# A decoder layer on one core: x given transposed too, weights laid out by chunks, plain x loaded later

## Chip, cores and metric

The kernel runs on one core of one Trainium2 chip. The metric is the device time of one execution in microseconds (us); several runs are made and their median is compared.

## What is computed

One layer with 256 positions and 1024 channels, all float32 at the interface. A pre-norm scales x by norm_in_g and by one over its root mean square; one wide projection w_in makes the inputs of two branches (block-sparse attention, which with 256 positions is plain causal attention of 8 heads, and gated linear attention, GLA), both are projected back, merged by sigmoid gates, projected by w_out, added to x and normed again.

```
h = rms_norm(x, norm_in_g)
(mq, mk, mv, mgate, gq, gk, gv, ggate, gfg, ga, gb) = split(h @ w_in)
oa = attention(rotary(mq), rotary(mk), mv) * silu(mgate);   ya = oa @ w_proj_a
ob = rms_norm(gla(gq/8, gk, gv, log_sigmoid(gfg @ w_fg2 + b_fg)/16)) * silu(ggate);   yb = ob @ w_proj_b
merged = sigmoid(ga + b_merge[0]) * ya + sigmoid(gb + b_merge[1]) * yb
out = rms_norm(x + merged @ w_out, norm_f_g)
```

## The kernel before

The 128 partitions hold channels (or positions), and every product keeps float32 precision by splitting both factors into a rounded part and a remainder (hi and lo for weights, xh and xl for x) and summing three matmuls: hi with xh, hi with xl, lo with xh. ScalarE makes each rounded part (a cast, line 179 for weights, line 256 for x), VectorE each remainder (line 180, line 257). The row's scale, one over the root mean square, is not applied to x but to the products' results.

Weights come in chunks in a fixed order (`load_to`, line 153; `split_to`, line 169). I call them by their product: **w0 to w7** are the eight chunks of the first product (the group "mg", kind K, 128 channels by 512 columns, 262 kB each, tile `first`), **g0 to g3** the four of the second ("gg", kind G, 541 kB each, tile `raw`), **q0 to q3** the four of the third ("gqk", 524 kB each), and so on. Raw chunks from g0 on have five buffers, hi and lo five each. x has eight pieces of 128 channels by 256 positions, **x0 to x7**.

All transfers of that stage are issued by SyncE's queue (SP), in program order. The framework gives the transfers eight counters in turn, so that a transfer is issued only once the one eight places before it has landed. x is loaded plain (positions on the partitions, tile `xt`), in rows of 512 bytes for x0 and x1 and of 1024 bytes later, ahead of the weight chunks that belong to them (lines 196 to 198). TensorE turns each piece by two transposes (`x_part`, line 252, tile `xp` in PSUM), and the casts read PSUM. norm_in_g arrives as rows and is turned by a transpose as well (tile `vp`, line 276), b_merge likewise in the middle of the second product (line 345).

The order of the instructions is written out by hand: the main loop over the groups (line 724) issues the products, and side generators such as `gates_mg` (line 338) are advanced at each `tick` when a clock that adds up matmul time says so. `squares` (line 266) sums the squares of x on ScalarE, `rms` (line 271) makes the row's scale `rs` on VectorE and GpSimd, `gates_mg` then makes two diagonal matrices of it (`diag`, line 343), broadcasts it over the partitions by matmuls with ones (line 349), copies the result to `rB` (line 351) and scales the first product by it (`mgz`, line 354). PSUM has four banks under the tag "small"; the third product's first bank, gqk, is the one that the first product's part mg0 leaves, so gqk's first matmul waits for the first `mgz` instruction, before and after the change.

Of the kernel before, what the change touches and what calls it, by code (L numbers as in the profile page):

```python
# [10 lines left out]
F32 = mybir.dt.float32  # L11
# [8 lines left out]
P = 128  # L20
# [55 lines left out]


@with_exitstack
def layer(ctx, tc, x, norm_in_g, w_in, b_merge, w_fg2, b_fg, gla_g, w_pa, w_pb, w_out, norm_f_g,
          rope, causal, sums, masks, out):  # L80
    nc = tc.nc
# [17 lines left out]
    def f32(ap):  # L99
        return ap.bitcast(F32)  # L100
# [9 lines left out]


    chunks = []
    groups = []

    def group(kind, name, src, c0, n, nk, step=2):
        ids = []
        if kind == "F":
            parts = [(c0 + p, 256, k0, 4) for p in range(0, n, 256) for k0 in range(0, nk, 4)]
        else:
            parts = [(c0, n, k0, step) for k0 in range(0, nk, step)]  # L120
        for c, w, k0, k in parts:
            ids.append(len(chunks))
            chunks.append(dict(src=src, c0=c, n=w, k0=k0, nk=k))
        groups.append(dict(kind=kind, name=name, ids=ids, nk=nk))

    group("K", "mg", w_in, C_MG, 512, KD, 1)
    group("G", "gg", w_in, C_GG, 528, KD)
    group("F", "gqk", w_in, C_GQ, 512, KD)
    group("F", "mq", w_in, C_MQ, 512, KD)
    group("F", "mk", w_in, C_MK, 512, KD)  # L130
    group("T", "mv", w_in, C_MV, 512, KD)
    group("T", "gv", w_in, C_GV, 512, KD)
    group("F", "ga0", w_in, C_GA, 512, KD)
    group("F", "ga1", w_in, C_GA + 512, 512, KD)
    group("F", "gb0", w_in, C_GB, 512, KD)
    group("F", "gb1", w_in, C_GB + 512, 512, KD)
    for h in range(2):
        group("F", f"pa{h}", w_pa, h * 512, 512, 4)
        group("F", f"pb{h}", w_pb, h * 512, 512, 4)
    oids = {}  # L140
    for half in range(2):
        for n in range(2):
            for k in range(4 * half, 4 * half + 4, 2):
                oids[n, k // 2] = len(chunks)
                chunks.append(dict(src=w_out, c0=n * 512, n=512, k0=k, nk=2))

# [6 lines left out]
    def load_to(n):  # L153
        while loaded[0] < min(len(chunks), n):
            c = chunks[loaded[0]]
            size = c["nk"] * c["n"]
            if loaded[0] < KD:
                c["raw"] = first[:, loaded[0], :]
            else:
                raw = ring.tile([P, WMAX], F32, name="raw", bufs=RAW)  # L160
                c["raw"] = raw[:, :size]
            nc.sync.dma_start(
                c["raw"].rearrange("p (k n) -> p k n", n=c["n"]),
                c["src"][c["k0"] * P:(c["k0"] + c["nk"]) * P, c["c0"]:c["c0"] + c["n"]].rearrange(
                    "(k p) n -> p k n", p=P),
            )
            loaded[0] += 1
# [38 lines left out]
    small_loads = [  # L206
        (brow, b_merge.rearrange("n (k p) -> (n k) p", p=P)),
        (flat(ropet), rope),
# [6 lines left out]
    ]  # L215
    load_to(KD + 2)
    for dst, src in small_loads[:6]:
        nc.sync.dma_start(dst, src)
# [44 lines left out]
    rB2 = rB[:, None, :].to_broadcast([P, 2, S])  # L263
    junk = one.tile([P, D], F32, name="junk", tag="m0")

    def squares(half):
        cs = slice(half * 512, half * 512 + 512)
        for t in range(NT):
            nc.scalar.activation(junk[:, :512], xt[:, t, cs], AF.Square, accum_out=ss[:, t, half:half + 1])

# [453 lines left out]
    for g in groups:  # L724
        ids, name = g["ids"], g["name"]
        if g["kind"] == "K":
            ps = [small(f"{name}{f}") for f in range(3)] + [bank(f"{name}3", "side", 1)]
            for i in ids:
                c = chunks[i]
                k = c["k0"]  # L730
                if k == 5:
                    squares(0)
                if k == 6:
                    squares(1)
                for f in range(4):
# [36 lines left out]
        elif g["kind"] == "F":  # L772
            src = {"pa": (oah, oal), "pb": (obh, obl)}.get(name[:2], (xh, xl))
            if name == "mq":
                for dst, given in small_loads[6:]:
                    nc.sync.dma_start(dst, given)
# [77 lines left out]
    for t in range(NT):  # L854
# [15 lines left out]

_INS = ["x", "norm_in_g", "w_in", "b_merge", "w_gla_fg2", "b_gla_fg", "gla_norm_g", "w_proj_a", "w_proj_b",
        "w_out", "norm_f_g"]
_ROWS = ("b_gla_fg", "gla_norm_g", "norm_f_g")


# [25 lines left out]
```

## Time and profile before

| what | value |
|---|---|
| median of 3 runs | 209.54 us (209.42 to 210.56) |
| the profiled execution | 209.73 us, its span 208.0 us |
| TensorE busy in the span | 198.8 us (96%) |
| VectorE, ScalarE busy | 141.6 us (68%), 122.6 us (59%) |
| moved by transfers | 35.39 MB, 170 GB/s over the span |

The span is the profiled part of that execution; 1.73 us of its time lie around it. Times in the rows further down are counted from the span's start. A matmul's busy time is modelled and overlaps the next one's, so the pace of TensorE is read from the distance of starts.

### The profile page before, as it was taken

Reading aid. Unit: us, or ns where it says so; the run is one execution under the profiler, and the core shown is the slowest. Engines: PE = TensorE matmul, PEld = TensorE weight load, DVE = VectorE, ACT = ScalarE, POOL = GpSimd, SP = SyncE. Lnnn points to the kernel's source line nnn. Section 1 sums busy time; section 2 is a strip of 40 time slices with the busy share of each in tenths; the row PEclk is TensorE's granted clock in tenths of the full one; section 3 lists DMA queues with packets and bytes.
Section 4 is the critical chain, followed back from the end, with each engine's and each line's share of the span. In section 5 each row is a group of like instructions: output and inputs, shape, how many; then the busy total and the mean of one; then the engine's idle time right before and its main releaser. Section 6 shows DMA issues by size and latency. Waiting matters only on the chain.

```text
span 208.0 us, 4231 instructions
## 1 busy us (share of the span) xinstructions
PE 198.8 (96%) x1683; PEld 182.4 (88%) x1683; DVE 141.6 (68%) x261; ACT 122.6 (59%) x205; POOL 32.5 (16%) x31
## 2 busy tenths in 40 slices
PE   7999999999999999998999999999999999999970
PEld 2899999899999988775789999999999999989870
DVE  1566778969545899989765556945393959755371
ACT  4369927871999984156775629846455554552251
POOL 2000025800214540103000000200010060420011
PEclk9999999999999999999999999999999999999998
DMA  5999896594364456660343563966344584600022
GB/s 144 349 379 323 238 310 211 135 296 149 101 199 117 145 158 191 193 218 14 107 123 86 182 193 114 294 210 198 108 151 154 168 301 135 204 4 2 0 101 101
DMA packets 28501, 35.39 MB, mean 170 GB/s; under 512 B 1305, under 2 KB 21442, under 8 KB 28482
## 3 DMA queue, kind: packets, MB, share of 16 engines
q1 hardware_dynamic: 28178, 34.60, 54.1%
q10 hardware_dynamic: 304, 0.53, 0.7%
q8 instruction: 13, 0.21, 0.4%
q14 instruction: 6, 0.05, 0.1%
HBM read 34.08 MB, written 1.05 MB: 169 GB/s over the span
## 4 chain that ended last, share of the span: by engine, by line
PE 67%; DVE 11%; ACT 11%; issue 5%; DMA 2%; SPq 1%; POOLq 0%; POOL 0%; ACTq 0%; DVEq 0%
PE ga L91 11%; PE gb L91 11%; PE po L91 8%; PE gg L91 6%; PE gqk L91 6%; PE pa L91 5%; PE pb L91 5%; DVE lo L180 4%; ACT hi L179 4%; PE mg L91 3%; ACT z L700 3%; PE mq L91 3%; DMA xt<-in_x_dram 2%; PE gv L91 2%; DVE EX L417 2%
## 5 line engine op out<-in xcount | busy, mean ns | idle before, releaser
L180 DVE TENSOR_TENSOR lo<-raw,hi 128x1024 fp32r<-128x1024 f32 (+1 forms) x56 | 70.4, 1269 | 23.5 <-ACT hi L179 23.5
L179 ACT CAST hi<-raw 128x1024 fp32r<-128x1024 f32 (+1 forms) x56 | 57.7, 1048 | 21.5 <-PE po L91 6.0
L91 PE MATMUL ga<-xh,hi 128*128 128x256 f32 x64 | 18.1, 283 | 0.0
L91 PE MATMUL gb<-xh,hi 128*128 128x256 f32 x64 | 18.1, 282 | 0.0
L91 PE MATMUL gb<-xh,lo 128*128 128x256 f32 x64 | 17.9, 279 | 0.0
L91 PE MATMUL gb<-xl,hi 128*128 128x256 f32 x64 | 17.9, 279 | 0.0
L91 PE MATMUL ga<-xh,lo 128*128 128x256 f32 x64 | 17.8, 278 | 0.0
L91 PE MATMUL ga<-xl,hi 128*128 128x256 f32 x64 | 17.8, 278 | 0.0
L91 PE MATMUL po<-hi,ml 128*128 128x512 f32 (+1 forms) x40 | 13.9, 347 | 0.0
L91 PE MATMUL po<-lo,mh 128*128 128x512 f32 (+1 forms) x40 | 13.8, 346 | 0.0
L91 PE MATMUL po<-hi,mh 128*128 128x512 f32 (+1 forms) x40 | 13.7, 343 | 0.0
L91 PEld LDWEIGHTS ga<-xh,hi 128*128 128x128 f32 x64 | 12.1, 189 | 0.5 <-issue 0.5
L558 ACT ACTIVATE sm<-sm,mx 128x128 f32<-128x128 f32 (+1 forms) x16 | 7.1, 444 | 8.7 <-DVE mx L553 8.6
L91 PEld LDWEIGHTS gb<-xh,lo 128*128 128x128 f32 x64 | 12.1, 189 | 0.0
L91 PEld LDWEIGHTS gb<-xh,hi 128*128 128x128 f32 x64 | 12.1, 189 | 0.0
L91 PEld LDWEIGHTS ga<-xl,hi 128*128 128x128 f32 x64 | 12.0, 188 | 0.0
L91 PEld LDWEIGHTS gb<-xl,hi 128*128 128x128 f32 x64 | 12.0, 188 | 0.0
L91 PEld LDWEIGHTS ga<-xh,lo 128*128 128x128 f32 x64 | 12.0, 188 | 0.0
L511 POOL TENSOR_TENSOR s<-s,mhalf 128x4 f32<-128x4 f32 x2 | 2.3, 1172 | 54.6 <-DVE s L510 54.6
L624 POOL TENSOR_TENSOR m<-m,sa 128x512 f32<-128x512 f32 x4 | 7.0, 1743 | 23.9 <-DVE m L622 22.0
L91 PE MATMUL mg<-xh,hi 128*128 128x256 f32 x32 | 10.3, 321 | 0.0
L91 PE MATMUL mg<-xl,hi 128*128 128x256 f32 x32 | 9.5, 296 | 0.0
(197 smaller groups left out, 605.7 us busy)
## 6 DMA issues: line engine op xcount, KB each, us to landing
raw<-in_w_in_dram SPq DMA_DIRECT2D x36, 512.0 KB, 3.7
raw<-in_w_out_dram SPq DMA_DIRECT2D x8, 512.0 KB, 4.8
raw<-in_w_in_dram SPq DMA_DIRECT2D x4, 528.0 KB, 6.0
first<-in_w_in_dram SPq DMA_DIRECT2D x8, 256.0 KB, 5.5
raw<-in_w_proj_a_dram SPq DMA_DIRECT2D x4, 512.0 KB, 3.5
raw<-in_w_proj_b_dram SPq DMA_DIRECT2D x4, 512.0 KB, 4.4
xt<-in_x_dram SPq DMA_DIRECT2D x3, 256.0 KB, 5.7
late<-in_norm_f_g_dram SPq DMA_DIRECT2D x1, 512.0 KB, 5.0
```

What stands on the lines that cost most here:

```text
L91: nc.tensor.matmul(out, lhsT, rhs, start=start, stop=stop)
L179: nc.scalar.copy(c["hi"], raw)
L180: nc.vector.tensor_sub(c["lo"], raw, f32(c["hi"]))
L417: nc.vector.tensor_mul(e, e, halves(src, LEVELS[l], which))
L511: nc.gpsimd.tensor_tensor(s4, s4, mhalf, op=OP.pow)
L558: nc.scalar.activation(sm[i][:, cs], sm[i][:, cs], AF.Exp, bias=mx[:, i, t:t + 1], scale=0.125, accum_out=den[:, i, t:t + 1])
L624: nc.gpsimd.tensor_add(m, m, cut(sg["ga"]))
L700: nc.scalar.copy(z[i:i + 32], p2[i ^ 32:(i ^ 32) + 32])
```

## The change

x is handed to the kernel a second time, transposed on the host side of the call (`xT`), norm_in_g and b_merge as ready columns (`columns`), and all weights as one array in which each chunk is contiguous (`weights`), so that a chunk's row per partition is 2048, 4224 or 4096 bytes instead of pieces of 2048, 2112, 2048 or 1024 bytes. The pieces of x for the first product come from `xT`; the 16 transposes of x, those of norm_in_g and b_merge and two copies of their results go. Plain x is still needed for the squares and the last sum; it is loaded as two transfers of 524 kB behind g0, g1 and g2. The squares stand on ScalarE behind the casts of g0 to g2, ahead of that of g3. Eight warm-up matmuls stand at the start instead of five and two.

```diff
+def laid_out(weights):
+    def chunk(src, c0, n, k0, nk, at):
+        w = weights[src][k0 * P:(k0 + nk) * P, c0:c0 + n]
+        return w.reshape(nk, P, n).transpose(1, 0, 2).reshape(-1)
+    return np.concatenate([chunk(**c) for c in plan()[0]])
...
             nc.sync.dma_start(
-                c["raw"].rearrange("p (k n) -> p k n", n=c["n"]),
-                c["src"][c["k0"] * P:(c["k0"] + c["nk"]) * P, c["c0"]:c["c0"] + c["n"]].rearrange(
-                    "(k p) n -> p k n", p=P),
-            )
+                c["raw"], weights[c["at"]:c["at"] + P * size].rearrange("(p n) -> p n", p=P))
...
+    vecs = one.tile([P, 24], F32, name="vecs")
+    nc.scalar.dma_start(vecs, columns)
+    xs = one.tile([P, KD, S], F32, name="xs", tag="m0")
+    xTr = xT.rearrange("(k p) s -> p k s", p=P)
     for k0, k1 in ((0, 1), (1, 2), (2, 4), (4, 6), (6, 8)):
-        nc.sync.dma_start(xt[:, :, k0 * P:k1 * P], xr[:, :, k0 * P:k1 * P])
+        nc.sync.dma_start(xs[:, k0:k1, :], xTr[:, k0:k1, :])
         load_to(k1)
...
-    load_to(KD + 2)
-    for dst, src in small_loads[:6]:
+    load_to(KD + 3)
+    for t in range(NT):
+        nc.sync.dma_start(xt[:, t], xr[:, t])
+    load_to(KD + 4)
+    for dst, src in small_loads[:5]:
         nc.sync.dma_start(dst, src)
     load_to(KD + RAW)
...
-    warm(5)
+    warm(8)
...
     def x_part(k):
-        xp = bank(f"xp{k}")[:, :S]
-        for t in range(NT):
-            transpose(xp[:, t * P:(t + 1) * P], xt[:, t, k * P:(k + 1) * P], ident)
-        nc.scalar.activation(xh[:, k, :], xp, AF.Copy, scale=vecs[:, k:k + 1])
-        nc.vector.scalar_tensor_tensor(xl[:, k, :], xp, vecs[:, k:k + 1], f32(xh[:, k, :]),
+        nc.scalar.activation(xh[:, k, :], xs[:, k, :], AF.Copy, scale=vecs[:, k:k + 1])
+        nc.vector.scalar_tensor_tensor(xl[:, k, :], xs[:, k, :], vecs[:, k:k + 1], f32(xh[:, k, :]),
...
     def gates_mg(ps):
+        yield 1.5
         rms()
...
-        transpose(ps[2][:, S:S + 16], brow, ident[:16, :16])
-        nc.vector.tensor_copy(vecs[:, 8:24], ps[2][:, S:S + 16])
...
-                if k == 5:
-                    squares(0)
-                if k == 6:
-                    squares(1)
-                for f in range(4):
-                    fs = slice(f * P, (f + 1) * P)
-                    if f == 2:
-                        if k + 2 < KD:
-                            x_part(k + 2)
-                        split_to(i + SPLIT - 1 if k > 3 else i + 3)
-                    three(ps[f][:, :S], c["hi"][:, 0, fs], c["lo"][:, 0, fs], xh[:, k, :], xl[:, k, :],
-                          k == 0, k == KD - 1)
+                if k + 2 < KD:
+                    x_part(k + 2)
+                split_to(i + SPLIT - 1 if k > 3 else i + 3)
+                parts = [(c["hi"], xh), (c["hi"], xl), (c["lo"], xh)]
+                todo = [(f, j) for f in range(4) for j in range(3)]
+                for f, j in sorted(todo, key=lambda n: n[::-1]) if k == 0 else todo:
+                    w, v = parts[j]
+                    mm(ps[f][:, :S], w[:, 0, f * P:(f + 1) * P], v[:, k, :], k == 0 and j == 0, k == KD - 1 and j == 2)
+            for half in range(2):
+                squares(half)
```

The queue of SyncE from g0 on, before; DMAHW0 to DMAHW7 are the eight counters, and a row waits for the last transfer on the one it names.

```order
L162 DMA raw<-in_w_in_dram 128x2x528 [waits DMAHW6_49]
L162 DMA raw<-in_w_in_dram 128x2x528 [waits DMAHW7_49]
L218 DMA brow<-in_b_merge_dram 16x128 [waits DMAHW0_49]
L218 DMA ropet<-in_rope_dram 128x512 [waits DMAHW1_49]
L218 DMA ggb<-in_gla_norm_g_dram 128x128 [waits DMAHW2_49]
L218 DMA fgw<-in_w_gla_fg_dram 16x256 [waits DMAHW3_49]
L218 DMA fgw<-in_b_gla_fg_dram 1x256 [waits DMAHW4_49]
L218 DMA sumsf<-in_sums_dram 128x512 [waits DMAHW5_49]
L162 DMA raw<-in_w_in_dram 128x2x528 [waits DMAHW6_49]
L162 DMA raw<-in_w_in_dram 128x2x528 [waits DMAHW7_49]
L162 DMA raw<-in_w_in_dram 128x4x256 [waits DMAHW0_49]
```

And in the change:

```order
L179 DMA raw<-in_weights_dram 128x1056 [waits DMAHW6_49]
L179 DMA raw<-in_weights_dram 128x1056 [waits DMAHW7_49]
L179 DMA raw<-in_weights_dram 128x1056 [waits DMAHW0_49]
L232 DMA xt<-in_x_dram 128x1024 [waits DMAHW1_49]
L232 DMA xt<-in_x_dram 128x1024 [waits DMAHW2_49]
L179 DMA raw<-in_weights_dram 128x1056 [waits DMAHW3_49]
L235 DMA ropet<-in_rope_dram 128x512 [waits DMAHW4_49]
L235 DMA ggb<-in_gla_norm_g_dram 128x128 [waits DMAHW5_49]
L235 DMA fgw<-in_w_gla_fg_dram 16x256 [waits DMAHW6_49]
L235 DMA fgw<-in_b_gla_fg_dram 1x256 [waits DMAHW7_49]
L235 DMA sumsf<-in_sums_dram 128x512 [waits DMAHW0_49]
L179 DMA raw<-in_weights_dram 128x1024 [waits DMAHW1_49]
```

Plain x (`xt`, two rows) stands between g2 and g3, and g2 now waits for a piece of x (DMAHW0) where it waited for g0 (DMAHW6).

TensorE at the broadcast of the row's scale (`diag` with ones), before; the lines cut out are the rest of gg:

```order
L91 MATMUL gg_356<-hi,xh 128x272
L91 MATMUL gg_356<-lo,xh 128x272
L91 MATMUL gg_356<-hi,xl 128x272
L96 MATMUL mg_185<-ident,brow 128x16
L91 MATMUL mg_186<-diag_424,ones 128x128
L91 MATMUL mg_186<-diag_425,ones 128x128
L91 MATMUL gg_353<-hi,xh 128x256
...
L91 MATMUL gg_356<-lo,xh 128x272
L91 MATMUL gg_356<-hi,xl 128x272
L91 MATMUL gqk<-xh,hi 128x256
L91 MATMUL gqk<-xl,hi 128x256
```

And in the change:

```order
L142 MATMUL gg_332<-hi,xl 128x256
L142 MATMUL gg_333<-hi,xh 128x272
L142 MATMUL gg_333<-lo,xh 128x272
L142 MATMUL gg_333<-hi,xl 128x272
L142 MATMUL mg_177<-diag_431,ones 128x128
L142 MATMUL mg_177<-diag_432,ones 128x128
L142 MATMUL gqk<-xh,hi 128x256
L142 MATMUL gqk<-xl,hi 128x256
```

The broadcast has moved from behind matmul 72 of the 96 of gg to behind the last, directly ahead of gqk; the turn of b_merge is gone.

ScalarE from the sixth piece of x to the copy of rB, before:

```order
L256 ACTIVATE xh<-xp_277,vecs 128x256
L179 CAST hi<-first 128x512 x2
L269 ACTIVATE junk,ss<-xt 128x512 x2
L256 ACTIVATE xh<-xp_304,vecs 128x256
L179 CAST hi<-raw 128x2x528
L269 ACTIVATE junk,ss<-xt 128x512 x2
L179 CAST hi<-raw 128x2x528 x3
L179 CAST hi<-raw 128x1024 x3
L351 COPY rB<-mg_186 128x256
```

And in the change:

```order
L264 ACTIVATE xh<-xs,vecs 128x256
L193 CAST hi<-first 128x512 x2
L264 ACTIVATE xh<-xs,vecs 128x256
L193 CAST hi<-raw 128x2x528 x3
L277 ACTIVATE junk,ss<-xt 128x512 x4
L193 CAST hi<-raw 128x2x528
L193 CAST hi<-raw 128x1024 x3
L356 COPY rB<-mg_177 128x256
```

The four squares (`junk,ss<-xt`) stand behind three casts of g chunks instead of around the first. On every engine the rows behind this place are the same ones in the same order as before, line numbers and the names of the weights' source apart.

## Rows read from the trace of the kernel before

**Rows 1.** The page, part 1: busy time of TensorE and its share of the span.

```profile
PE 198.8 (96%) x1683; PEld 182.4 (88%) x1683; DVE 141.6 (68%) x261; ACT 122.6 (59%) x205; POOL 32.5 (16%) x31
```

**Rows 2.** The chain of waits that ended last: start, duration (us), what.

```profile
51.85 0.58 ACT z L700
```

**Rows 3.** Timeline of TensorE, the start: start, us, instruction [idle before <-what ended it].

```profile
5.67 0.77 PE L91 MATMUL mg<-xh,hi 128*128 128x256 f32 x1
...
6.67 0.41 PE L91 MATMUL mg<-xh,hi 128*128 128x256 f32 x1
6.88 0.41 PE L91 MATMUL mg<-xl,hi 128*128 128x256 f32 x1
...
7.87 0.69 PE L96 MATMUL xp<-ident,xt 128*128 128x128 f32 x2 [0.36 <-DMA xt<-in_x_dram]
```

**Rows 4.** Timeline of ScalarE: casts of the first two weight chunks.

```profile
4.23 0.62 ACT L179 CAST hi<-first 128x512 fp32r<-128x512 f32 x1 [1.35 <-DMA first<-in_w_in_dram]
...
6.77 0.62 ACT L179 CAST hi<-first 128x512 fp32r<-128x512 f32 x1 [1.55 <-DMA first<-in_w_in_dram]
```

**Rows 5.** Timeline of VectorE: the remainder of the second chunk.

```profile
7.43 0.69 DVE L180 TENSOR_TENSOR lo<-first,hi 128x512 fp32r<-128x512 f32 x1 [1.46 <-ACT hi L179]
```

**Rows 6.** Timeline of SyncE's queue: two issues that wait for landings.

```profile
8.49 1.06 SPq L162 DMA_DIRECT2D raw<-in_w_in_dram  x2
...
14.80 27.29 SPq L162 DMA_DIRECT2D raw<-in_w_in_dram  x13
```

**Rows 7.** Timeline of TensorE: matmuls of the first product at full pace.

```profile
15.42 0.28 PE L91 MATMUL mg<-xh,hi 128*128 128x256 f32 x1
...
16.36 0.28 PE L91 MATMUL mg<-xh,lo 128*128 128x256 f32 x1
```

**Rows 8.** Timeline of TensorE: the second product, the broadcast, the third's start.

```profile
20.81 0.38 PE L91 MATMUL gg<-lo,xh 128*128 128x256 f32 x1
...
29.39 0.28 PE L91 MATMUL gg<-hi,xl 128*128 128x272 f32 x1
...
29.76 0.71 PE L91 MATMUL mg<-diag,ones 128*128 128x128 f32 x4
30.23 0.36 PE L91 MATMUL gg<-hi,xh 128*128 128x256 f32 x1
...
33.22 0.28 PE L91 MATMUL gqk<-xh,hi 128*128 128x256 f32 x1
```

**Rows 9.** Busy time by stretch: busy us (count) of PE, PEld, DVE, ACT, POOL; PEclk; DMA share; GB/s.

```profile
8.00:16.00 8.00, 8.00 (x66) 8.00 (x67) 5.45 (x11) 4.68 (x10) 0.00 (x0) 1.00 1.06 382
9.00:10.00 1.00, 1.00 (x11) 1.00 (x11) 0.88 (x2) 0.58 (x2) 0.00 (x0) 1.00 1.05 395
2.00:3.00 1.00, 1.00 (x4) 0.30 (x2) 0.00 (x0) 0.87 (x2) 0.01 (x1) 1.00 0.97 196
```

**Rows 10.** Timeline of VectorE: from g3's remainder to the scaling by rB.

```profile
24.19 1.25 DVE L180 TENSOR_TENSOR lo<-raw,hi 128x1056 fp32r<-128x1056 f32 x1
...
27.49 0.48 DVE L343 TENSOR_SCALAR diag<-ident,rs 128x128 f32<-128x128 f32 x2 [0.61 <-POOL rs L274]
...
31.09 0.74 DVE L354 TENSOR_TENSOR mgz<-mg,rB 128x256 f32<-128x256 f32 x2
```

**Rows 11.** Timeline of ScalarE: squares, a cast of 1024 columns, rB, gfT.

```profile
16.66 0.63 ACT L269 ACTIVATE junk<-xt 128x512 f32<-128x512 f32 x1
...
17.42 0.63 ACT L269 ACTIVATE junk<-xt 128x512 f32<-128x512 f32 x1
...
24.96 1.05 ACT L179 CAST hi<-raw 128x1024 fp32r<-128x1024 f32 x1 [0.25 <-DMA raw<-in_w_in_dram]
...
30.51 0.37 ACT L351 COPY rB<-mg 128x256 f32<-128x256 f32 x1 [2.54 <-PE mg L91]
...
36.81 0.36 ACT L371 COPY gfT<-gft 16x256 f32<-16x256 f32 x1
```

**Rows 12.** Timeline of ScalarE: the wait ahead of the rotary copies.

```profile
51.85 2.35 ACT L700 COPY z<-mq 32x512 f32<-32x512 f32 x4 [4.33 <-PE mq L91]
```

More of the change, by code (lines that the diff above doesn't have):

```diff
@@ L75, in constants, with plan, group, layer @@
     }
+def plan():
+    chunks = []
+    groups = []
+    def group(kind, name, src, c0, n, nk, step=2):
+        ids = []
+        if kind == "F":
+            parts = [(c0 + p, 256, k0, 4) for p in range(0, n, 256) for k0 in range(0, nk, 4)]
+        else:
+            parts = [(c0, n, k0, step) for k0 in range(0, nk, step)]
+        for c, w, k0, k in parts:
+            ids.append(len(chunks))
+            chunks.append(dict(src=src, c0=c, n=w, k0=k0, nk=k))
+        groups.append(dict(kind=kind, name=name, ids=ids, nk=nk))
+    group("K", "mg", "w_in", C_MG, 512, KD, 1)
+    group("G", "gg", "w_in", C_GG, 528, KD)
+    group("F", "gqk", "w_in", C_GQ, 512, KD)
+    group("F", "mq", "w_in", C_MQ, 512, KD)
+    group("F", "mk", "w_in", C_MK, 512, KD)
+    group("T", "mv", "w_in", C_MV, 512, KD)
+    group("T", "gv", "w_in", C_GV, 512, KD)
+    group("F", "ga0", "w_in", C_GA, 512, KD)
+    group("F", "ga1", "w_in", C_GA + 512, 512, KD)
+    group("F", "gb0", "w_in", C_GB, 512, KD)
+    group("F", "gb1", "w_in", C_GB + 512, 512, KD)
+    for h in range(2):
+        group("F", f"pa{h}", "w_proj_a", h * 512, 512, 4)
+        group("F", f"pb{h}", "w_proj_b", h * 512, 512, 4)
+    oids = {}
+    for half in range(2):
+        for n in range(2):
+            for k in range(4 * half, 4 * half + 4, 2):
+                oids[n, k // 2] = len(chunks)
+                chunks.append(dict(src="w_out", c0=n * 512, n=512, k0=k, nk=2))
+    at = 0
+    for c in chunks:
+        c["at"] = at
+        at += P * c["nk"] * c["n"]
+    return chunks, groups, oids
+def laid_out(weights):
[3 more added lines that the diff above has]
+    return np.concatenate([chunk(**c) for c in plan()[0]])
 @with_exitstack
-def layer(ctx, tc, x, norm_in_g, w_in, b_merge, w_fg2, b_fg, gla_g, w_pa, w_pb, w_out, norm_f_g,
-          rope, causal, sums, masks, out):
+def layer(ctx, tc, x, xT, columns, weights, w_fg2, b_fg, gla_g, norm_f_g, rope, causal, sums, masks, out):
     nc = tc.nc
@@ L109, in small @@
         return bank(name, "small", 4)
[L112 to L145, printed above, removed]
+    chunks, groups, oids = plan()
     WMAX = 1056
@@ L774, in layer @@
             if name == "mq":
[L775 removed]
+                for dst, given in small_loads[5:]:
                     nc.sync.dma_start(dst, given)
@@ L883, in given @@
     def given(name, a):
+        a = np.ascontiguousarray(a)
         arrays[f"in_{name}_dram"] = a
         args.append(nc.dram_tensor(f"in_{name}_dram", a.shape, mybir.dt.from_np(a.dtype), kind="ExternalInput").ap())
-    for name in _INS:
-        a = np.ascontiguousarray(inputs[name])
-        if name == "norm_f_g":
-            a = a[None]
-        elif name not in _ROWS:
-            a = a[0]
-        given(name, np.ascontiguousarray(a))
+    put = {name: np.asarray(a) for name, a in inputs.items()}
+    x = put["x"][0]
+    given("x", x)
+    given("xT", x.T)
+    given("columns", np.concatenate([put["norm_in_g"].reshape(KD, P), put["b_merge"].reshape(2 * KD, P)]).T)
+    given("weights", laid_out({name: put[name][0] for name in ("w_in", "w_proj_a", "w_proj_b", "w_out")}))
+    given("w_gla_fg2", put["w_gla_fg2"][0])
+    given("b_gla_fg", put["b_gla_fg"])
+    given("gla_norm_g", put["gla_norm_g"])
+    given("norm_f_g", put["norm_f_g"][None])
     for name, a in constants().items():
-        given(name, np.ascontiguousarray(a))
+        given(name, a)
     args.append(nc.dram_tensor("out_0_dram", (S, D), F32, kind="ExternalOutput").ap())
```

25 lines of the change are left out of this document (6 added, 19 removed).

## Prediction

> **What bounds the kernel now.** I read the busy shares first: TensorE is busy 96% of the span [rows 1], so an edit pays only where it takes time from TensorE or a stall out of its stream. The chain of waits then tells where TensorE is not what ends last: at 51.85 us it crosses from TensorE to ScalarE [rows 2], which had been waiting for the product mq [rows 12]. The change touches only the first 33 us, so I followed those on the timelines, engine by engine, for the point at which all later work begins: the first matmul of gqk at 33.22 [rows 8]. The reader should see three things there.
>
> First, the start is paced by landings. The casts of w0 and w1 wait for transfers until 4.23 and 6.77 [rows 4], the first real matmul starts at 5.67, and at 7.87 TensorE still waits for a piece of x that it is to turn, in the middle of its first chunk [rows 3].
>
> Second, its matmuls start 0.21 us apart at first, 0.94 / 8 = 0.1175 apart later [rows 3, 7]: 256 columns in those times are the 1.2 and the 2.4 GHz level, although the column of the granted clock reads 1.00 in all stretches shown [rows 9].
>
> Third, between the last gg matmul at 29.39 and gqk stand the broadcast of the row's scale, 0.47 us to the next matmul, and 24 matmuls of gg [rows 8]. These hide what happens behind the broadcast: ScalarE copies rB at 30.51 and VectorE scales mg0 from 31.09 [rows 10, 11], the instruction that gqk waits for.
>
> **The change, part by part.**
>
> *Start.* w0's hi is ready at 4.23 + 0.62 = 4.85 [rows 4], and the first chunk's matmuls no longer stop for x: I take 4.9 where it was 5.67. The eight warm-ups, of 512 columns and so 0.425 each at the slow pace, end at 1.2 + 3.4 = 4.6, before it. This wants xs0 and the columns by about 3.7. The old piece was there by then; the columns' landing is not shown. Between landing in time (no cost) and landing 0.6 late (0.6, were that chunk the limit) I take none, since the next chunk waits for w1 anyway: the 12 matmuls end at 4.9 + 12 x 0.2125 = 7.45 even at the slow pace. w1's hi is ready at 6.77 + 0.62 = 7.39, its lo at 7.43 + 0.69 = 8.12 [rows 4, 5]. Two matmuls can go, the third needs the lo, and ten remain: 8.12 + 10 x 0.1175 = 9.3 (up to 0.3 more if the slow pace lasts to 8.9 as now).
>
> *w2 and on.* g0's issue at 8.49 waited for w2's landing (the transfer eight places before it) [rows 6]; cast and remainder, 0.62 + 0.69, put its lo at 9.8. So the third chunk ends at 9.8 + 1.18 = 10.98. From there five chunks of 12 x 0.1175 = 1.41 run unbroken, to 18.0. The turns of x between the chunks are gone with it.
>
> *Packets.* x0 and x1 came in rows of 512 bytes. The stretch in which they start moves 196 GB/s at a DMA share of 0.97, one with 2048-byte weight rows 395 at 1.05 [rows 9]. 262 kB cost 1.33 us at the one rate, 0.66 at the other; with rows of 1024 bytes I take half the difference, 0.3 us, on all landings (bounds 0 and 0.7). By the Trainium skill, "DMA: Bandwidth & Descriptors", Specifications, 512 bytes is already enough for line rate; by that this term is 0 and the sum 1.8 in place of 2.1. The rows speak against it. gg then starts at 18.0 - 0.3 = 17.7, its second matmul at 17.8 in place of 20.81 [rows 8]: **3.0 us earlier**.
>
> *gg.* The second to the 72nd matmul started within 29.39 - 20.81 = 8.58 us [rows 8], 0.1226 apart; 96 take 11.8, and TensorE reaches the broadcast at 29.5. g0 landed by 14.80 [rows 6] (g2's issue waited for it); its hi and lo, 1.05 and 1.25 [rows 11, 10], are ready by 17.1, in time. The turn of b_merge, 0.16, is saved.
>
> *The broadcast, moved.* It now stands directly ahead of gqk. From its start rB is copied 0.75 later and takes 0.37, then the first of the two mgz instructions in 0.74 takes about 0.4 [rows 8, 10, 11]: 29.5 + 0.75 + 0.37 + 0.4 plus hand-overs of 0.05 gives gqk at 31.1. So about 1.1 us in which TensorE waits are new; 24 matmuls of gg covered them before. gqk starts 33.22 - 31.1 = **2.1 us earlier**.
>
> *The row's scale* must be ready by 29.5, and here plain x comes in. From g0's landing to q0's, 3.80 MB must pass: three g chunks 1.62, plain x 1.05, five small tables 0.61, q0 0.52. At 382 GB/s [rows 9] this is 9.95 us: q0 lands at 14.5 + 9.95 = 24.4. Its hi and lo end at 24.4 + 1.05 + 1.25 = 26.7 [rows 10, 11], behind which `rms` stands on VectorE. From the end of such a lo (25.44) to the end of both diagonals (27.97) it was 2.5 us [rows 10]: ready at 29.2, hardly before TensorE arrives. The margin is 0.3. For it speaks that g and x rows of 4 kB and more may move faster than the 2 kB rows of that stretch. The squares end before: the second half of plain x lands near 20, three more squares at 0.76 [rows 11] end near 22.3, g3's cast at 23.4, and TensorE wants g3's lo only at 17.7 + 72 x 0.1226 = 26.5. q1 lands 1.4 behind q0; its lo (28.1) is in front of the diagonals and no later than they are.
>
> *Behind the third product's start* nothing changes its order. rB itself is copied at 30.25 in place of 30.51, and what hangs on it all but keeps its time: gfT is done at 36.81 + 0.36 - 0.26 = 36.9 [rows 11]. TensorE wants it 48 matmuls and two turns behind gqk's start, 31.1 + 48 x 0.1175 + 0.2 = 36.9. Ahead of the rotary copies ScalarE idles 4.33 us until TensorE brings mq [rows 12], so up to 4.3 us of TensorE's gain pass there, and from there the chain keeps its distances. ScalarE and VectorE read as many elements of x as before, from SBUF instead of PSUM. I cost that at nothing: the copy of 256 columns from PSUM takes 0.37 [rows 11], and with a weight cast of 0.62 even the double of it hides under the 1.41 of a chunk.
>
> *Sum.* 3.0 at gg, 0.2 from b_merge's turn, less 1.1 for the new wait: 2.1. The profiled execution of 209.73 would take 207.6. It lies 0.19 above the median of the runs, so I predict **207.4 us** against 209.54.
>
> **The rivals.** *The scale comes late.* Each us by which q0 lands later than 24.7 moves gqk by as much, for the diagonals are ready 0.3 ahead. Against it: the queue holds work throughout, because each issue waits for a landing eight transfers back. A rate a twentieth under the 382 GB/s of the rows, 363, puts q0 at 14.5 + 10.5 = 25.0, the gain at 1.8 and the time at 207.7; a tenth under it, 344, at 25.5, 1.3 and 208.2. The trace moves 382 over 8 us, so I give it 0.10. The Trainium skill, same page, "Where 436 GB/s comes from", names about 358 GB/s as what the HBM side allows a core; by that this rival holds, and the 382 of the trace speaks against it. A scale late by one to two us for another reason (small tables, a slow engine among 16) gives a gain of 0.4 to 1.4, a time of 208.1 to 209.1: 0.10.
>
> *Slower.* The same chain, from the point at which q0 lands at 26.8: 4.8 to the diagonals and 1.6 from the broadcast to gqk then end at 33.2, with nothing gained; slower than can be measured from 27.8 on, a rate of 3.80 / 13.3 = 286 GB/s from g0 on. The place is plain x between g2 and g3: 1.05 MB on the path of the scale that were there from the start before. At 29 the time is 211.7. For it speaks only that the queue moved 196 with short rows; chance 0.06.
>
> *More.* Contiguous chunks land 1 us sooner from w1 on than I take: gg starts at 16.7, q0 lands at 23.4, the diagonals are ready at 28.2, and gqk starts at 30.1. A gain of 3.1, 206.4: 0.10. For it speaks that the rate was lowest where rows were shortest [rows 9].
>
> *The gain does not pass.* If gfT or the decay factors behind it hold TensorE until its old time, all is lost again before mq and the time is 209.5. The margin at gfT is none, but what is late there is late by tenths; 0.06.
>
> **How the numbers follow.** The forecast, a gain of 1.7 to 2.7, gets 0.58. The range from 206.0 to 208.8 takes in the earlier landings up to a gain of 3.5 and the late scale down to 0.7; it leaves out the slower case, the lost gain and the outer parts of two others, 0.20. About 0.5%, 1.05 us, is what a measurement of this kernel can tell from no change. Faster by more: 0.58 + 0.10 + 0.10 + 0.03 of the late scale = 0.81. Within it: 0.07 + 0.06 = 0.13. Slower: 0.06.
>
> **What would show it.** On TensorE: first mg matmul near 4.9, gg near 17.7 with no turns between, a gap of about 1.1 us between broadcast and gqk that VectorE's mgz ends, gqk near 31.1, mq and everything behind it 2.1 earlier. On ScalarE: squares near 20 to 22.3; a wait for DMA ahead of q0's cast near 24.4. It is wrong if the broadcast itself waits for the diagonals by more than half a us, if gg starts later than 18.5, or if the idle ahead of the rotary copies shrinks while these stay at 51.85.

## The result and the profile after

The changed kernel takes 207.35 us (median of 4 runs, 206.99 to 207.41), the kernel before 209.58 beside it: a ratio of 0.987, 95% interval 0.984 to 0.990. The profiled execution took 207.39 us with a span of 205.6, against 209.73 and 208.0. 2.34 us of it are to be explained, against 2.1 forecast.

TensorE's busy time and its share, part 1 of the page of the changed kernel, answers to [rows 1]: 3.8 us less, the share hardly lower.

```profile
PE 195.0 (95%) x1666; PEld 179.0 (87%) x1666; DVE 141.2 (69%) x259; ACT 123.4 (60%) x205; POOL 38.1 (19%) x31
```

The timeline of TensorE in the changed kernel (start, us, instruction, in brackets the idle time before it and what ended it) shows the new stretch from the start to the third product, beside [rows 3, 8]:

```profile
4.47 1.19 PE L142 MATMUL mg<-xh,hi 128*128 128x256 f32 x4
...
7.42 0.39 PE L142 MATMUL mg<-xh,lo 128*128 128x256 f32 x1 [0.22 <-DVE lo L194]
...
17.17 0.28 PE L142 MATMUL gg<-hi,xh 128*128 128x256 f32 x1
17.29 0.28 PE L142 MATMUL gg<-lo,xh 128*128 128x256 f32 x1
...
28.68 0.28 PE L142 MATMUL gg<-hi,xl 128*128 128x272 f32 x1
29.75 0.71 PE L142 MATMUL mg<-diag,ones 128*128 128x128 f32 x4 [0.79 <-DVE diag L350]
31.41 0.38 PE L142 MATMUL gqk<-xh,hi 128*128 128x256 f32 x1 [0.95 <-DVE mgz L359]
...
35.30 0.28 PE L142 MATMUL gqk<-xl,hi 128*128 128x256 f32 x1
...
37.11 0.28 PE L142 MATMUL gqk<-xh,lo 128*128 128x256 f32 x1
...
55.63 0.28 PE L142 MATMUL mk<-xh,hi 128*128 128x256 f32 x1
```

Two more lines of the kernel before, behind those of [rows 8]: a later matmul of gqk and the first one of mk.

```profile
35.93 0.28 PE L91 MATMUL gqk<-xh,lo 128*128 128x256 f32 x1
...
57.99 0.28 PE L91 MATMUL mk<-xh,hi 128*128 128x256 f32 x1
```

The reader sees four things. The second matmul of gg starts at 17.29 in place of 20.81, 3.5 us earlier, and TensorE could start the broadcast at 29.75 - 0.79 = 28.96. There it waits, as was not forecast, 0.79 us for the diagonals, and then, as was, 0.95 for mgz. So gqk starts at 31.41, only 1.81 us earlier. Yet mk, the fifth product, starts 2.36 earlier than the 57.99 of before, and everything behind it keeps that. Between gqk and mk 0.55 us were gained by something that the prediction does not have.

VectorE of the changed kernel shows why the diagonals are late, beside [rows 10]: `rms` (rs) stands behind the remainder of q0, and that behind q0's landing.

```profile
23.74 1.26 DVE L194 TENSOR_TENSOR lo<-raw,hi 128x1056 fp32r<-128x1056 f32 x1 [4.63 <-ACT hi L193]
26.16 1.23 DVE L194 TENSOR_TENSOR lo<-raw,hi 128x1024 fp32r<-128x1024 f32 x1 [1.17 <-ACT hi L193]
27.30 0.15 DVE L280 TENSOR_TENSOR rs<-ss 128x2 f32<-128x2 f32 x1
...
29.41 0.48 DVE L350 TENSOR_SCALAR diag<-ident,rs 128x128 f32<-128x128 f32 x2 [0.61 <-POOL rs L282]
29.81 1.21 DVE L194 TENSOR_TENSOR lo<-raw,hi 128x1024 fp32r<-128x1024 f32 x1
30.95 0.74 DVE L359 TENSOR_TENSOR mgz<-mg,rB 128x256 f32<-128x256 f32 x2
```

ScalarE of the changed kernel, beside [rows 4, 11, 12]: w1's cast at 6.02 in place of 6.77, the squares behind two waits for plain x, q0's cast at 25.08, and the rotary copies 2.28 us earlier with 2.19 of idle time left ahead of them, where it was 4.33.

```profile
6.02 0.62 ACT L193 CAST hi<-first 128x512 fp32r<-128x512 f32 x1 [0.92 <-DMA first<-in_weights_dram]
...
19.48 0.63 ACT L277 ACTIVATE junk<-xt 128x512 f32<-128x512 f32 x1 [1.67 <-DMA xt<-in_x_dram]
...
20.79 0.63 ACT L277 ACTIVATE junk<-xt 128x512 f32<-128x512 f32 x1 [0.58 <-DMA xt<-in_x_dram]
...
25.08 1.05 ACT L193 CAST hi<-raw 128x1024 fp32r<-128x1024 f32 x1 [1.38 <-DVE lo L194]
...
36.66 0.35 ACT L376 COPY gfT<-gft 16x256 f32<-16x256 f32 x1
...
49.57 2.35 ACT L705 COPY z<-mq 32x512 f32<-32x512 f32 x4 [2.19 <-PE mq L142]
```

The bracket of 25.08 names the remainder of g3, which ends at 25.00 and which that cast does not need; q0 itself landed at 24.98 by the trace. That it is the landing which counts is seen in the runs below with the old weight transfers and with four warm-ups: there g3's remainder ended 0.4 and 0.5 us ahead of q0's cast, and the cast began 0.1 behind the landing all the same. By stretch (the columns of [rows 9]), the changed kernel moves 286 GB/s where x starts, in place of 196, and 393 in place of 382 later. From 14 to 25 us, between the landings of g0 and q0, it moves 375:

```profile
2.00:3.00 1.00, 1.00 (x4) 0.43 (x3) 0.00 (x0) 0.65 (x2) 0.01 (x1) 1.00 0.94 286
8.00:16.00 8.00, 8.00 (x71) 8.00 (x70) 6.81 (x12) 6.71 (x13) 0.00 (x0) 1.00 1.03 393
14.00:25.00 11.00, 11.00 (x94) 11.00 (x93) 5.53 (x6) 6.87 (x12) 0.00 (x0) 1.00 1.01 375
```

### The profile page after: what moved, and what is told of

The parts are those of the page before. It is cut to its first block, busy times and chain, and to the rows that moved or that the text cites. A ratio compares the mean times of both kernels' runs of the same rounds, so it can differ in the third digit from the quotient of the medians.

```text
span 205.6 us, 4197 instructions
## 1 busy us (share of the span) xinstructions
PE 195.0 (95%) x1666; PEld 179.0 (87%) x1666; DVE 141.2 (69%) x259; ACT 123.4 (60%) x205; POOL 38.1 (19%) x31
## 4 chain that ended last, share of the span: by engine, by line
PE 58%; DVE 12%; ACT 11%; DMA 8%; issue 6%; SPq 2%; POOL 1%; POOLq 0%; DVEq 0%; ACTq 0%
PE ga L142 11%; PE gb L142 11%; PE po L142 8%; PE gqk L142 6%; PE pa L142 5%; PE pb L142 5%; DVE lo L194 5%; DMA xt<-in_x_dram 5%; ACT hi L193 4%; ACT z L705 3%; DMA first<-in_weights_dram 3%; PE mq L142 3%; PE gv L142 2%; DVE EX L422 2%; ACT EX L405 2%
## 5 line engine op out<-in xcount | busy, mean ns | idle before, releaser
L709 POOL TENSOR_TENSOR kT<-kT,z 128x512 f32<-128x512 f32 x2 | 10.5, 5234 | 7.2 <-DVE z L708 7.2
L142 PE MATMUL gqk<-xh,hi 128*128 128x256 f32 x32 | 9.2, 286 | 1.0 <-DVE mgz L359 1.0
```

Of the source, the lines that this page charges most:

```text
L142: nc.tensor.matmul(out, lhsT, rhs, start=start, stop=stop)
L709: nc.gpsimd.tensor_add(dst, dst, z)
```

## The experiments

Two questions were open. Why is the scale late, its place on VectorE or the transfers? And where do 0.55 us come from behind gqk? In the timelines, matmuls of 256 columns come 118 ns apart in gqk, mq and mk of before (23 distances from 33.22 to 35.93), and 113 ns apart in gqk and the first two thirds of mq of the changed kernel (16 distances from 35.30 to 37.11). **Theory P**: the quicker pace comes with the new standstill of TensorE ahead of gqk. **Theory L**: it comes with the new layout.

**rms ahead of q0's remainder.**

```diff
     def gates_mg(ps):
-        yield 1.5
         rms()
-        yield 3.5
+        yield 6.0
```

> One edit to the changed kernel: rms stands on VectorE ahead of the remainder of q0 instead of behind it; broadcast and diagonals keep their places. Theory (the scale was late by its place in VectorE's order: it stood behind a remainder that waits for q0's landing at 25.1): rs is ready near 26.9 in place of 29.4, the diagonals run right behind the remainder of q1 at 28.7, the 0.79 us wait ahead of the broadcast shrinks to 0.2 or less, the remainder of q2 and with it the first mgz end 0.7 sooner, gqk starts at 30.7 in place of 31.41, and the time falls by 0.5 to 0.7 us to about 206.8. Rival (the transfers set the end, whatever the order on VectorE): the remainders of q1 and q2 are no earlier, gqk stays at 31.3 to 31.4, 207.3 us.

Measured: 207.16 us, ratio 0.988 (0.986 to 0.991), and gqk at 31.29, not at 30.7. VectorE of this run:

```profile
24.97 0.15 DVE L280 TENSOR_TENSOR rs<-ss 128x2 f32<-128x2 f32 x1
...
28.63 0.48 DVE L349 TENSOR_SCALAR diag<-ident,rs 128x128 f32<-128x128 f32 x2
...
30.81 0.42 DVE L358 TENSOR_TENSOR mgz<-mg,rB 128x256 f32<-128x256 f32 x1 [0.57 <-ACT rB L355]
```

The theory holds for the scale: q0's cast began at 25.15, as late as before, yet rs came 2.3 us and the diagonals 0.8 earlier, and TensorE did not wait for them. The gain in time was missed because in this trace w1 landed later, gg started at 18.16 and TensorE itself came to the broadcast only at 29.77. The start varies from one execution to the next, a point to which the repeated run below returns.

**The wait ahead of gqk covered.** rms and the diagonals come before the remainders of q0 and q1, the broadcast 12 matmuls earlier, and the remainder of q2 is held back.

```diff
     def gates_mg(ps):
-        yield 1.5
         rms()
         yield 3.5
...
-        yield 1.5
+        yield 3.0
         r = ps[3][:, S:]
...
         nc.scalar.copy(rB, r)
+        split_to(KD + 7, hold=True)
...
-        split_to(i + SPLIT - 1)
+        split_to(i + SPLIT - 1 - (i == KD + 3))
...
                 nc.vector.tensor_scalar(gfs[:, t, :], ps[t, 1][:, 256:272], rs[:, t:t + 1], None, op0=OP.mult)
+            for one_lo in held:
+                nc.vector.tensor_sub(*one_lo)
```

> The changed kernel with the wait ahead of gqk covered: rms and diagonals ahead of the remainders of q0 and q1, the broadcast 12 matmuls of gg earlier, and the remainder of q2 behind mgz and gfs instead of ahead of them (its cast behind rB). Both theories say that the waits of 0.79 and 0.95 us ahead of broadcast and gqk nearly go and gqk starts at 29.6 to 29.9. They differ behind it. Theory P (TensorE's matmuls fall into a quicker pace, 113 ns in place of 118, by the way in which the stream is entered after a standstill): without the wait gqk and the first part of mq run at 118 ns again, which gives 0.5 to 0.7 us back, and the time falls by only 0.9 to 1.2 us, to about 206.3. Theory L (the quicker pace in gqk and mq comes from the contiguous chunks): 113 ns stays and the time falls by 1.5 to 1.7 us, to about 205.7. A third outcome, the decay gates' gfT becomes the wait: TensorE stops ahead of fg, and less than 0.8 us is gained.

Measured: 206.30 us, ratio 0.984 (0.981 to 0.987). TensorE of this run:

```profile
27.86 0.60 PE L142 MATMUL mg<-diag,ones 128*128 128x128 f32 x4
28.22 0.36 PE L142 MATMUL gg<-hi,xh 128*128 128x256 f32 x1
...
29.75 0.28 PE L142 MATMUL gqk<-xh,hi 128*128 128x256 f32 x1
...
32.46 0.28 PE L142 MATMUL gqk<-xh,lo 128*128 128x256 f32 x1
...
54.52 0.28 PE L142 MATMUL mk<-xh,hi 128*128 128x256 f32 x1
```

No wait is left, gqk starts 1.66 us earlier than in the changed kernel, at 29.75, though gg started half a us later. Its matmuls are 118 ns apart again (23 distances from 29.75 to 32.46), in the new layout. At mk 1.11 of the 1.66 remain: 0.55 are given back. That is theory P, and against L.

**Weights read in strided pieces; the layout alone.** The first is the changed kernel with the old weight transfers, the second the kernel before with the new ones.

```diff
-                c["raw"], weights[c["at"]:c["at"] + P * size].rearrange("(p n) -> p n", p=P))
+                c["raw"].rearrange("p (k n) -> p k n", n=c["n"]),
+                weights[c["src"]][c["k0"] * P:(c["k0"] + c["nk"]) * P, c["c0"]:c["c0"] + c["n"]].rearrange(
+                    "(k p) n -> p k n", p=P),
+            )
```

> The changed kernel with the weights read from the original arrays in strided pieces, x still given transposed. Theory (the gain at the start comes from x: its turns gone, its rows of 512 bytes gone, and plain x out of the way of w0 to w7, whose rows have 2048 bytes in both layouts): w1 and w2 land within 0.2 of 6.0 and 7.4, gg starts within 0.3 of 17.17; only q0 to q3, whose pieces are 1024 bytes again, come up to 0.5 later, and the time is 207.4 to 207.9. Rival (contiguous chunks make the landings sooner): w1 and w2 land 0.5 or more later, gg starts at 17.7 or later, and the time is 208.0 or more. If the quicker pace in gqk and mq is due to the layout, both are back at 118 ns here.

> The kernel before with the weights laid out by chunks, x still turned on TensorE. Theory (the layout is worth little at the start, where TensorE waits for x and for its turns): gg starts within 0.4 of 20.45, gqk within 0.4 of 33.22, and the time falls by 0 to 0.4 us, to 209.2 to 209.6. Rival (layout carries the gain): 208.5 or less. If the layout makes the quicker pace, gqk and mq run at 113 ns here and 0.7 us is gained behind gqk.

Measured: strided 207.99 us (ratio 0.993, 0.990 to 0.997), its profiled execution 207.58 with gg at 17.70, gqk at 31.57 and q0's cast at 25.13; layout alone 210.34 us (1.004, 1.001 to 1.006). So the layout by itself gains nothing; the run came out 0.1 to 0.6% slower, not in the expected 209.2 to 209.6. With x transposed the layout's worth is between 0.2 (the profiled executions) and 0.6 us (the medians), which these intervals do not separate from none. The strided run met the marks of the rival (w2's cast 0.54 later, gg at 17.70, 207.99) rather than those of the theory, but the marks were too narrow: over the traces with this start gg alone varies from 17.17 to 18.16. The pace is 113 ns in the strided gqk and 118 in that of the layout alone: L falls twice.

Neither run tests the term "packets" of the prediction, which is about the rows of x: the strided run keeps rows of 1024 bytes, the layout alone those of 512. From 2 to 3 us the traces with 1024 bytes move 221 to 352 GB/s, the three with 512 bytes 175 to 212; but other things differ there as well, and the lowest of them, 175 with the layout alone, comes at a DMA share of 0.55, so that the length of rows can't be all of it. The term by itself is not shown. The Trainium skill, "DMA: Bandwidth & Descriptors", Specifications, has 512 bytes as enough for line rate. The weights, in pieces of 1024 bytes and more in either layout, agree with it; for the rows of x these runs do not decide.

The profiled execution with the layout alone took 212.13 us, and the timeline of TensorE shows what held this one up:

```profile
8.51 0.69 PE L148 MATMUL xp<-ident,xt 128*128 128x128 f32 x2 [0.95 <-DMA xt<-in_x_dram]
...
12.62 0.41 PE L143 MATMUL mg<-xh,hi 128*128 128x256 f32 x1
12.84 0.41 PE L143 MATMUL mg<-xl,hi 128*128 128x256 f32 x1
```

Behind a wait of 0.95 us its matmuls stay 213 ns apart, the 1.2 GHz level, until 13.2 us, and gg starts at 22.86 in place of 20.45. That is where the warm-ups come in.

**Four warm-up matmuls in place of eight.**

```diff
-    warm(8)
+    warm(4)
```

> The changed kernel with four warm-up matmuls in place of eight. In the traces so far the matmuls of the first product come 213 ns apart until 8.9 us in the kernel before (until 13.2 in the run with the layout alone, 212.1 us), but only until 5.0 to 5.5 with eight warm-ups. Theory C (the eight warm-ups, which keep TensorE at work up to the first product, bring TensorE's quick level early): with four, which end near 2.9 us, matmuls stay 213 ns apart to 7.5 or later, the first chunks take up to 1.2 us more each, gg starts at 18.5 or later (17.2 to 18.2 with eight), and the time rises by 0.3 to 2 us, as far as the 0.8 us for which TensorE waits for the scale does not hide it. Rival (the level rises as early without them, or w1 and w2 are waited for anyway): gg at 17.2 to 18.2 and 207.0 to 207.6 us.

Measured: 207.83 us, ratio 0.989 (0.984 to 0.993). TensorE of this run, the end of the 213 ns:

```profile
10.17 0.41 PE L142 MATMUL mg<-xh,lo 128*128 128x256 f32 x1
10.38 0.40 PE L142 MATMUL mg<-xh,hi 128*128 128x256 f32 x1
...
10.86 0.28 PE L142 MATMUL mg<-xh,hi 128*128 128x256 f32 x1
10.97 0.28 PE L142 MATMUL mg<-xl,hi 128*128 128x256 f32 x1
```

Theory C holds: TensorE stood still for 1.48 us between the warm-ups and the first product, the quick level comes at 10.7 instead of 5 to 6.6, and gg starts at 18.68, later than in any trace with eight and the same transfers. But gqk starts at 31.81, between the changed kernel's two traces (31.41 above, 32.20 below): in those two the late scale had taken up what the earlier start gained. The time alone, whose interval overlaps that of the changed kernel, would not have shown it.

**A short wait put back into the covered version.**

```diff
-        for f in range(4):
-            nc.vector.tensor_mul(mgz[:, f, :], ps[f][:, :S], rB)
         nc.vector.tensor_mul(ropet, ropet, rB2)
         nc.vector.tensor_copy(sumsr, sumsf)
+        for f in range(4):
+            nc.vector.tensor_mul(mgz[:, f, :], ps[f][:, :S], rB)
```

> The covered version (206.3 us, no wait ahead of gqk, gqk and mq at 118 ns) with one edit: the two other products of VectorE (ropet, sumsr, together about 0.95 us) stand ahead of mgz, so that TensorE waits some 0.3 to 0.6 us ahead of gqk. Theory P (a standstill directly ahead of gqk is what brings the 113 ns): gqk and the first part of mq run at 113 to 115 ns, 0.65 us is given back, and mk starts no later than with the cover, time 206.0 to 206.4. Rival (the pace came from something else in the changed kernel's order): 118 ns stays, the wait is lost in full, and the time is 206.6 to 206.9.

Measured: 207.04 us (0.984, 0.980 to 0.989), the profiled execution 206.70.

```profile
30.70 0.36 PE L142 MATMUL gqk<-xh,hi 128*128 128x256 f32 x1 [0.50 <-DVE mgz L366]
...
31.36 0.28 PE L142 MATMUL gqk<-xh,lo 128*128 128x256 f32 x1
...
33.40 0.28 PE L142 MATMUL gqk<-xh,lo 128*128 128x256 f32 x1
...
54.88 0.28 PE L142 MATMUL mk<-xh,hi 128*128 128x256 f32 x1
```

The pace is as P has it: 113 ns in gqk (18 distances from 31.36 to 33.40), where the covered version has 118. The broadcast stands 12 matmuls ahead of gqk here, so that it is the standstill and not the broadcast that goes with the pace. gqk starts 0.95 later than there (0.28 of it gg's later start), mk 0.36. The time was missed, above both expectations: the median is not under the covered version's, so a wait is not worth making for the pace it brings.

**Plain x ahead of g0.**

```diff
-    load_to(KD + 3)
     for t in range(NT):
         nc.sync.dma_start(xt[:, t], xr[:, t])
+    load_to(KD + 3)
```

> The changed kernel with plain x loaded directly behind w7, ahead of g0 to g2, instead of behind them. Theory (its place behind g2 is worth what it keeps out of the way of g0): 1.05 MB at 390 GB/s move g0 to g2 by 2.7 us, the remainder of g0 ends at 19.0, gg starts in earnest at 19.0, 1.7 later, TensorE reaches the broadcast at 30.6, after the scale is ready, and gqk starts at 32.3, 0.9 later than 31.41: about 208.3 us. Rival (the scale alone sets gqk, and g0 comes in time either way): gqk at 31.4, 207.4.

Measured: 208.72 us (0.994, 0.991 to 0.997).

```profile
19.43 0.39 PE L142 MATMUL gg<-lo,xh 128*128 128x256 f32 x1 [0.91 <-DVE lo L194]
...
32.80 0.28 PE L142 MATMUL gqk<-xl,hi 128*128 128x256 f32 x1
...
35.39 0.28 PE L142 MATMUL gqk<-xh,lo 128*128 128x256 f32 x1
```

gg starts in earnest at 19.43 and gqk at 32.58, 1.17 later. The theory holds; plain x behind g2 is worth more than a us. This run is also an exception to P as worded: TensorE stood still for 0.92 us ahead of gqk, and yet the first 24 matmuls came 118 ns apart (22 distances from 32.80 to 35.39). The 113 ns began only behind the turns for gfT.

**The wide matmuls halved.**

```diff
-                mm(e, gs[:, c % 2, c // 2, ct * P:(ct + 1) * P], sumsr, start=True, stop=True)
+                for s0 in (0, 256):
+                    mm(e[:, s0:s0 + 256], gs[:, c % 2, c // 2, ct * P:(ct + 1) * P], sumsr[:, s0:s0 + 256],
+                       start=True, stop=True)
```

> The changed kernel with each of the eight matmuls of 512 columns for the decay factors (e) made as two of 256. In its trace the 113 ns pace ends at 51.41 us with the first e and does not return in mq and mk. Theory Q (the matmul of 512 columns ends the quick pace): mq keeps 113 to 114 ns to its end and mk runs at 113 too, mk takes 0.3 to 0.4 us less, and 0.4 to 0.5 us is gained, to 206.9. Rival (any foreign matmul in the stream ends it): mq falls to 118 ns at the same place, mk stays at 118, and the time is 207.3 to 207.5.

Measured: 207.34 us (0.987, 0.982 to 0.991). Q falls: the 113 ns end with the first pair of halves, at 50.8 us, and mk runs at 118 ns. In this run q0 came earlier (its cast at 24.46) and TensorE did not wait for the scale, so the trace also shows the changed kernel's order without its first wait: gqk at 30.80, again 6.3 us behind q0's cast (25.08 to 31.41 in the changed kernel).

**The changed and the covered kernel again, side by side; and the wait put into the kernel before.** The last is one edit to the kernel before:

```diff
         rms()
-        yield 3.5
+        yield 6.0
```

> The changed kernel once more, for its spread and beside the covered version on one chip. Over the traces so far in which the start is the changed kernel's own, the cast of w1 began between 5.95 and 6.95 and gg between 17.17 and 18.16, so the first trace was among the early ones. Theory (the scale and the wait ahead of gqk take up most of that spread): gg anywhere from 17.2 to 18.2, gqk at 30.8 to 31.8, gqk and the first part of mq at 113 to 115 ns, median 207.0 to 207.7 us. Rival (the start passes to the end in full): gqk moves with gg, 14.2 us behind it, and the time spreads by as much as the start.

> The covered version once more, on the same chip as the changed kernel. Theory P: no wait at broadcast or gqk, gqk and mq at 118 ns, gqk 1 to 1.7 us earlier than in the changed kernel, of which 0.5 to 0.6 is given back by mk; median 0.6 to 1.2 us under the changed kernel's. Rival (its first result was a lucky start): within 0.4 us of the changed kernel.

> The kernel before with one edit: the broadcast stands directly ahead of gqk, as in the changed kernel, instead of 24 matmuls earlier; all else is as before. Both theories: a new wait of 0.9 to 1.1 us ahead of gqk, which starts near 34.2. Theory P (the wait itself brings the 113 ns pace): gqk and the first part of mq run at 113 to 115 ns, where they had 118, mk starts only 0.3 to 0.5 later than 57.99, and the kernel is 0.3 to 0.5 us slower than before. Rival (the pace belongs to the changed kernel): 118 ns stays and it is 0.9 to 1.1 us slower.

Measured on one chip: the changed kernel 207.53 us (12 runs, 206.94 to 209.94; 0.990, 0.987 to 0.993), the covered one 206.16 (6 runs, 205.75 to 206.81; 0.982, 0.978 to 0.986), the kernel before with the wait 210.41 against 209.45 (1.003, 1.000 to 1.006). The covered version beats both kernels, the changed one by 1.4 us, more than the 0.6 to 1.2 expected, and its two results, 206.30 and 206.16, agree. It still waited 0.64 us at its broadcast here, where q0's cast came at 25.78; its gqk, 12 matmuls of gg later, kept 118 ns, so that a standstill further ahead did not bring the quick pace. For the changed kernel the median came as expected, but not the profiled execution: gqk started at 32.20, which is 14.1 us behind gg, as the rival has it, and also 6.3 us behind q0's cast at 25.87. The run with halves, 13.2 behind gg and again 6.3 behind q0's cast, speaks for the scale as what gqk follows.

The kernel before with the wait is the clean test of P, for nothing but the place of the broadcast, with its diagonals and the turn of b_merge, is changed:

```profile
36.55 0.38 PE L91 MATMUL gqk<-xh,hi 128*128 128x256 f32 x1 [0.92 <-DVE mgz L354]
...
36.99 0.28 PE L91 MATMUL gqk<-xh,hi 128*128 128x256 f32 x1
...
39.26 0.28 PE L91 MATMUL gqk<-xh,lo 128*128 128x256 f32 x1
```

Its gqk runs at 113 ns (20 distances from 36.99 to 39.26). (It starts so late because this execution, 212.55 us, stayed at 213 ns until 12.9, like the one with the layout alone.) The distance from gqk's to mk's first matmul, worked out from the starts in each trace, sums it up:

| trace | wait ahead of gqk | gqk | mk | distance |
|---|---|---|---|---|
| before | none | 33.22 | 57.99 | 24.77 |
| layout alone | none | 35.62 | 60.39 | 24.77 |
| covered, and again | none | 29.75, 30.33 | 54.52, 55.10 | 24.77, 24.77 |
| changed | 0.95 | 31.41 | 55.63 | 24.22 |
| rms first | 0.92 | 31.29 | 55.50 | 24.21 |
| strided | 0.95 | 31.57 | 55.77 | 24.20 |
| short wait | 0.50 | 30.70 | 54.88 | 24.18 |
| before with the wait | 0.92 | 36.55 | 60.74 | 24.19 |
| four warm-ups | 0.92 | 31.81 | 56.01 | 24.20 |
| halves | 0.94 | 30.80 | 55.02 | 24.22 |
| plain x ahead of g0 | 0.92 | 32.58 | 56.87 | 24.29 |
| changed, again | 0.95 | 32.20 | 58.12 | 25.92 |

The lines above the last say 24.2 to 24.3 with a wait and 24.77 without, in both layouts and in both orders. The last one is told of below. In time the kernel before with the wait is 0.1 to 1.2 us slower by its interval, which holds both expectations; it is the distance that tells them apart.

## Why the prediction came out

The time was forecast at 207.4 and measured at 207.35. That the number fits so well is luck: in the profiled execution three terms were off, by 0.6, 0.8 and 0.55 us, and cancel to within 0.3. It was right that the new start brings TensorE to the broadcast at least 3 us earlier, that the broadcast then adds a wait of about 1.1, and that what is gained at gqk passes to the end.

*Start.* "gg then starts at 18.0 - 0.3 = 17.7" was 17.17 in the profiled execution. Over the eight traces with this start it began between 17.17 and 18.16, 17.73 on average, and w1's cast between 5.40 and 6.95. So the step holds on average; that executions spread by a us around it was not in it. It also rests on matmuls at 0.1175 from w1's remainder on, for which the prediction allowed 0.3 us. Eight warm-ups made that true; with four the 213 ns lasted to 10.7. The prediction counted only when the warm-ups end. Its term of 0.3 for the rows of x is tested by no run alone. What the experiments single out of the earlier start are the warm-ups, about 1 us at gg, and the place of plain x, 2.1 us (gg in earnest at 17.29 against 19.43); the turns of x were not put back by themselves.

*The row's scale* is the first step that failed: "ready at 29.2, hardly before TensorE arrives. The margin is 0.3." The chain from q0's remainder to the diagonals did take 2.5 us (27.4 to 29.9), and the order on VectorE was as described. What was mis-sized is the time from g0's landing to q0's. The 3.80 MB at 382 GB/s were to take 9.95 us; it was 11.0, from 14.0 (0.5 earlier than taken) to 24.98 (24.4 forecast). Over eight traces q0's cast began at 25.0 on average (23.92 to 25.87). The rate is not the main reason, for the 375 GB/s from 14 to 25 us are 2% under it and make 4.1 MB: more than the bytes counted moved before q0 was complete. What moved ahead was not found out; behind g2, in the same order of transfers, q0 landed 6.8 to 8.3 us later from trace to trace. The 382 itself was taken from an earlier stretch; in the kernel before the stretch from 14 to 25 us moved 287 GB/s, which the prediction did not look at. The rival "a rate a twentieth under" gave q0 at 25.0 and a gain of 1.8 at gqk, and these numbers came, 24.98 and 1.81, though not by its reason. As TensorE also came 0.5 earlier than forecast, the margin of 0.3 became a wait of 0.79. By the prediction's own sign, a wait of more than half a us at the broadcast, this step was wrong.

*The broadcast, moved*: of "about 1.1 us in which TensorE waits", 0.95 and the slower first matmul were found. The length was right. Its price was not: the wait brings the 113 ns pace and with it 0.55 us back by mk. This is the second failed step, "gqk 2.1 earlier, and everything behind it 2.1 earlier". In the profiled execution the sum reads: 33.22 - 0.47 - 28.96 = 3.79 us of work done earlier (3.2 forecast), less 0.79 for the scale (0), less 1.19 from the broadcast's end by 0.47 to gqk (1.1), plus 0.55 of pace (0): 2.36, and 2.34 at the end.

*Behind the third product's start* the gain passes, as forecast: gfT was done in time, and the idle time ahead of the rotary copies took up the rest. The slower rival did not come. Its chain, from q0's landing to the diagonals, is the one that TensorE waited for; that plain x is what made q0 late was not tested by itself.

## What to carry to other kernels

A small instruction that stands in order behind one which waits for a transfer inherits that transfer's lateness: ask of each member of a critical chain what is ahead of it on its engine, not only what it reads. The price of a wait on the busiest engine need not be its length (0.95 us, less the 0.55 that came back, cost 0.4 here); compare the distance of two later products in traces with and without it. And where one wait hides another, a change can do its work and not show in the time: with four warm-ups gg was 1 us later than the average with eight and the kernel only 0.3 to 0.5 us slower, which the intervals do not separate from none.

## What was not expected of the hardware

Matmuls of 256 columns have two distances at the quick level, 113 and 118 ns. Of the nine traces with a standstill of 0.50 to 0.95 us directly ahead of gqk, seven show the quicker one from gqk's first matmuls on; with plain x ahead of g0 it began behind the turns for gfT, and in the trace told of next behind the matmuls fg. None of the four traces without the standstill had it anywhere in gqk, mq or mk. Where it had begun it came back behind those turns and matmuls, and it ended for good with the first e in mq, whole or halved. What in TensorE makes the two was not found out.

The other surprise is a risk that the waits carry. In the repeated run of the changed kernel the profiled execution took 209.94 us against a median of 207.53, with waits of 0.65 and 0.95 us ahead of broadcast and gqk. Behind them:

```profile
32.54 0.35 PE L142 MATMUL gqk<-xh,lo 128*128 128x256 f32 x1
32.69 0.41 PE L142 MATMUL gqk<-xh,hi 128*128 128x256 f32 x1
32.91 0.42 PE L142 MATMUL gqk<-xl,hi 128*128 128x256 f32 x1
```

And by stretch (columns as in [rows 9]):

```profile
28.00:32.00 4.00, 2.60 (x20) 2.19 (x18) 3.35 (x8) 1.62 (x3) 1.63 (x1) 1.00 0.96 336
32.00:36.00 4.00, 3.80 (x19) 3.80 (x20) 3.73 (x12) 2.83 (x6) 1.70 (x1) 0.58 0.68 247
```

The granted clock is 0.58 in the mean of 32 to 36 us, the matmuls are 213 ns apart, the 1.2 GHz level, from 32.7 to 36.0, and the distance to mk is 25.92: 1.7 us lost. TensorE had stood still for 1.6 of the 2.3 us up to gqk's start. The changed kernel's first profile, with 0.79 and 0.95, shows no such fall, so that the waits alone do not decide it. The Trainium skill, "TensorE: Matmul & The Clock Gate", HAM oscillation, tells of a kernel whose waits for transfers put the array back to its low clock each time. This one trace is in line with it, by 1.7 us, though its waits are for VectorE; that they are the cause is not shown. The covered version's ten runs stayed between 205.67 and 206.81, the changed kernel's sixteen between 206.94 and 209.94; that the other long ones have the same cause was not shown.
